# Which weight halves get their low part by accumulating DMA, by GpSimd or by VectorE, and when the conditioning loads are queued

## The chip, the cores and the metric

One core of one Trainium2 chip. The metric is the device time of one execution in microseconds. Three runs of the kernel before took 2086.33, 2087.24 and 2091.59 us (median 2087.24).

## The reference

Two decoder layers on a sequence of 256 tokens with model width 1024. Each layer has a conditioning part, a mixer and an expert part:

```python
mod = cond @ w_mod[l] + b_mod[l]                       # 6 x 1024 numbers from the conditioning vector
h = rms_norm(x, norm1_g[l]) * (1.0 + sc1) + sh1
x = x + g1 * hybrid_mixer(h, w_in[l], w_out[l], ...)   # attention, two convolutions, spatial gating
h = rms_norm(x, norm2_g[l]) * (1.0 + sc2) + sh2
x = x + g2 * peer_ffn(h, ...)                          # 8 heads, 16 of 128*128 one-neuron experts each
```

`peer_ffn` computes queries (`h @ wq`), scores them against 2 x 128 keys per head, takes the 16 best pairs per head and adds up `gate * gelu(h . u[e]) * v[e]` over the chosen experts e. All data are float32.

## The kernel before, in words

**Weights as a stream.** All weights of a layer are a list of tiles of 128 x 1024 float32 (512 KB): 20 of `win`, 8 of `wout`, 16 of `wq`, 128 of `u`, 128 of `v`. The kernel computes all 16384 experts densely: the "up" stage multiplies h with every `u` tile and takes gelu, gates (zero for experts not chosen) are multiplied in, and the "down" stage multiplies with every `v` tile.

**High and low parts.** TensorE multiplies in a shortened format (fp32r), so that each tile is cut into `hi` (the tile rounded) and `lo` (tile minus `hi`), and each product is three matmuls: hi*hi, hi*lo, lo*hi (`mm3`, L362 to L364 in the mixer, query and up stages; L928 in the down stage). The third one, L364, is the first to need `lo`.

**Class `Stream`** does this, by halves of 512 columns. `load` (L175) queues the 512 KB load of `raw` on SyncE; there are 4 `raw` buffers. `split_halves` (L179 to L210) makes `hi` and `lo` of one half; there are 6 buffers of each, three tiles' worth. It chooses one of three ways, per tile (both halves alike):

- "dve": ScalarE copies `raw` to `hi` (L200), VectorE subtracts (L202).
- "pool": ScalarE copies `raw` to `hi` (L200), GpSimd subtracts (L202 too).
- "dma": ScalarE writes `-raw`, rounded to fp32r, to `lo` (L196); a DMA that GpSimd issues adds `raw` to it (L197), which leaves the low part; ScalarE copies `raw` to `hi` (L198).

The share of tiles that goes each way is set stage by stage in `self.stream.share`: `MIXSHARE` in the mixer and query stages, `SHARE[0]` in the first half of up (64 tiles), `SHARE[1]` in the second half of up, `SHARE[2]` in the first half of down, `SHARE[3]` in the second half of down, and `{"dma": 1.0}` for the first two tiles of the program. What neither "dma" nor "pool" takes is VectorE's. The split runs 5 halves ahead of the multiplication (`AHEAD`).

**What runs beside the matmuls.** Class `Background` places slices of other work between the tiles: with each tile it advances its own clock by `STEP`, and a slice is emitted when VectorE's planned work is not more than `LEAD` ahead. A VectorE low part is charged with `LOCOST` = 0.6 us (`charge`). In the first half of up this other work is the choice of the experts (`topk`: MAX8, FIND_INDEX8, MATCH_REPLACE8 at L788 to L792, the 256 candidate sums per head at L799, one-hot products at L815 to L821), and in layer 0 also 16 conditioning chunks. In the second half of up and the first half of down it is the gates (`gates`: VectorE compares and products at L866 to L874, matmuls at L879, L887). In the second half of down of layer 0 it is 40 conditioning chunks of layer 1.

**Conditioning** (`mod_tiles`): a chunk is a load of 128 x 1025 float32 (L280, SyncE's queue, as the weights) and one VectorE SCALAR_TENSOR_TENSOR with a sum (L286). With n buffers, n-1 loads are queued first; after the instruction for chunk i the load of chunk i+n-1 follows, into the buffer of chunk i-1, and then the generator yields.

**Order.** Emission order is a priority. The framework's scheduler lets an instruction that it takes to be ready pass one that still waits; on each engine and queue the order that it fixed is then kept at run time, so that a waiting entry holds up what stands behind it, on SyncE's queue and on GpSimd's too.

At the start (`start`, L1021 on) GpSimd multiplies x by its norm (L1060, 8 instructions) and makes the low parts of h (L1073, 7 of 8); VectorE runs 16 conditioning chunks; the first two `win` tiles are split in between.

Of the kernel before, what the change touches and what calls it, by code (L numbers as in the profile page):

```python
# [15 lines left out]
ALU = mybir.AluOpType  # L16
# [21 lines left out]
MODCOST = 1.2  # L38
LOCOST = 0.6
HALF = D // 2  # L40
# [5 lines left out]
KTAKE = 3  # L46
CONVRANK = 2.5
PACE = (1.0, 2.6)
SHARE = ({"dma": 0.3, "pool": 0.7}, {"dma": 0.25}, {"dma": 0.2}, {"dma": 0.1})
NCOL = 94  # L50
NROW = 64 + 256 + 256 + 128
CH_SLICES = (4, 3, 0, 1, 7, 6, 5)
# [101 lines left out]
class Stream:  # L154
# [24 lines left out]
    def split_halves(self, upto):  # L179
        nc = self.nc  # L180
        while self.ns <= min(upto, 2 * len(self.aps) - 1):
            n, k = divmod(self.ns, 2)
            if k == 0:
                self.load(n)
                self.parts[n] = ([], [])
                self.by = "dve"
                for way in ("dma", "pool"):
                    self.acc[way] += self.share.get(way, 0.0)
                    if self.by == "dve" and self.acc[way] >= 1.0:
                        self.acc[way] -= 1.0  # L190
                        self.by = way
            raw = self.raw[n][:, HALF * k:HALF * k + HALF]
            hi = self.pool.tile([P, HALF], F32R, name="hi", tag="hi", bufs=6)
            lo = self.pool.tile([P, HALF], F32R, name="lo", tag="lo", bufs=6)
            if self.by == "dma":
                nc.scalar.activation(out=lo, in_=raw, func=AF.Copy, scale=-1.0)  # L196
                nc.gpsimd.dma_start(out=lo, in_=raw, accum_op=ALU.add)  # L197
                nc.scalar.activation(out=hi, in_=raw, func=AF.Copy)  # L198
            else:
                nc.scalar.activation(out=hi, in_=raw, func=AF.Copy)  # L200
                eng = nc.gpsimd if self.by == "pool" else nc.vector
                eng.tensor_tensor(out=lo, in0=raw, in1=hi.bitcast(F32), op=ALU.subtract)  # L202
                if self.by == "dve":
                    self.bg.charge(LOCOST)
            self.parts[n][0].append(hi)
            self.parts[n][1].append(lo)
            self.ns += 1
            if k:
                del self.raw[n]
                self.load(n + self.depth)  # L210
# [9 lines left out]
class Trunk:  # L220
# [52 lines left out]
    def mod_tiles(self, l, chunks, sc, bufs, tail=True, pace=0.0):  # L273

        nc = self.nc
        n = len(bufs)

        def load(i):
            if i < len(chunks):
                nc.sync.dma_start(out=bufs[i % n], in_=self.io["wmod"][l, chunks[i]])  # L280

        for i in range(n - 1):
            load(i)
        for i, j in enumerate(chunks):
            w = bufs[i % n]
            nc.vector.scalar_tensor_tensor(out=w, in0=w, scalar=1.0, in1=sc, op0=ALU.mult, op1=ALU.mult,  # L286
                                           accum_out=self.modT[:, l, j:j + 1])
            load(i + n - 1)
            yield MODCOST, pace
        for j0 in (8, 32):  # L290
            if tail and j0 in chunks:
                m = self.modT[:, l, j0:j0 + 8]
                g = self.col(l, 0 if j0 == 8 else 8, 8)
                nc.vector.scalar_tensor_tensor(out=m, in0=m, scalar=1.0, in1=g, op0=ALU.add, op1=ALU.mult)
                yield 0.2
# [64 lines left out]
    def mm3(self, out, whi, wlo, hhi, hlo, start, stop):  # L360
        mm = self.nc.tensor.matmul
        mm(out, whi, hhi, start=start, stop=False)  # L362
        mm(out, whi, hlo, start=False, stop=False)  # L363
        mm(out, wlo, hhi, start=False, stop=stop)  # L364
# [574 lines left out]
    def experts(self, l, area):  # L939
# [13 lines left out]
        acts = [self.big(32, T) for _ in range(2)]  # L953
        self.stream.share = SHARE[0]
        run = self.up(hb, acts)
        next(run)
        self.stream.share = SHARE[1]
        acts += [self.big(32, T) for _ in range(2)]
# [5 lines left out]
        for i in range(2):  # L964
            self.bg.add(self.gates(1, acts[2:4], i, kept))
        self.stream.share = SHARE[2]
        run = self.down(acts)
        next(run)
        self.stream.share = SHARE[3]
        self.m = Carve(self.big(), self.big())  # L970
# [50 lines left out]
    def start(self):  # L1021

        nc, io, one = self.nc, self.io, self.one
        self.cols = one.tile([P, L * NCOL + 8], F32, name="cols")
        self.ident = one.tile([P, P], F32, name="ident")
        self.xT = one.tile([P, NC, T], F32, name="xT")
        self.ones = one.tile([P, P], F32, name="ones")
        self.eps = one.tile([P, 1], F32, name="eps")
        self.iota = one.tile([P, P, 2], FP16, name="iota")
        self.modT = one.tile([P, L, 48], F32, name="modT")  # L1030
        self.idx = one.tile([P, 2, T], FP16, name="idx")
        self.gidx = one.tile([P, 2 * T], FP16, name="gidx")
        nc.vector.memset(self.ones, 1.0)
        nc.vector.memset(self.eps, EPS)
        self.neghalf = one.tile([P, 8], F32, name="neghalf")
        nc.vector.memset(self.neghalf, -0.5)
        self.m = m = Carve(self.big(), self.big())
        self.m2 = Carve(self.big())
        row = m.take(D)
        nc.sync.dma_start(out=row[0:1], in_=io["crow"])  # L1040
        nc.sync.dma_start(out=self.cols, in_=io["cols"])
        for i in range(2):
            nc.sync.dma_start(out=self.xT[:, 4 * i:4 * i + 4], in_=io["xT"][:, 4 * i:4 * i + 4])
        cr = self.m2.take(D + 1)
        for i in range(2):
            b = self.bank()
            nc.tensor.matmul(b, self.ones[0:1], row[0:1, 512 * i:512 * i + 512], start=True, stop=True)
            nc.scalar.activation(out=cr[:, 512 * i:512 * i + 512], in_=b, func=AF.Silu)
        nc.vector.memset(cr[:, D:D + 1], 1.0)
        bufs = [self.m2.take(D + 1) for _ in range(6)]  # L1050
        mods = self.mod_tiles(0, [j for c in range(NC) for j in (c, 8 + c)], cr, bufs, tail=False)
        next(mods)
        rs = self.rstd_d(m)
        self.stream.depth = 0
        self.stream.share = {"dma": 1.0}
        self.stream.split(1)
        r = self.bias_rows()
        xa, a = m.take(NC, T), m.take(2, T)
        for c in range(NC):
            nc.gpsimd.tensor_tensor(out=xa[:, c], in0=self.xT[:, c], in1=rs, op=ALU.mult)  # L1060
        hhi, hlo = hb = [self.mid(NC, T, dt=F32R) for _ in range(2)]
        for c in range(NC):
            for _ in range(2 if c else 1):
                next(mods)
            sh, sc = self.modT[:, 0, c:c + 1], self.modT[:, 0, 8 + c:9 + c]
            nc.vector.tensor_scalar(out=sc, in0=sc, scalar1=1.0, scalar2=self.col(0, c, 1), op0=ALU.add, op1=ALU.mult)
            nc.scalar.activation(out=hhi[:, c], in_=xa[:, c], func=AF.Identity, scale=sc, bias=sh)
            if c < NC - 1:
                nc.scalar.activation(out=a[:, c % 2], in_=xa[:, c], func=AF.Identity, scale=sc, bias=sh)
            else:  # L1070
                nc.vector.tensor_scalar(out=a[:, c % 2], in0=xa[:, c], scalar1=sc, scalar2=sh, op0=ALU.mult, op1=ALU.add)
            eng = nc.gpsimd if c < NC - 1 else nc.vector
            eng.tensor_tensor(out=hlo[:, c], in0=a[:, c % 2], in1=hhi[:, c].bitcast(F32), op=ALU.subtract)  # L1073
        for _ in mods:
            pass
        self.stream.load(3)
        self.stream.depth = self.stream.RAW
        nc.sync.dma_start(out=self.ident, in_=io["consts"][:, 0:P])
        m.reset()
        self.bias = m.take(4, 256)  # L1080
        self.table = self.bg.add(self.bias_table(r), rank=-1)
        self.bg.pump(0.1)
        self.mods = self.mod_tiles(0, list(range(16, 40)), cr, bufs[0:WBUFS])
        return hb
# [101 lines left out]
```

## Time and profile before

| what | value |
|---|---|
| median of three runs | 2087.24 us |
| the profiled execution's own time | 2079.62 us |
| its span | 2077.8 us |
| mean granted TensorE clock | 0.961 |
| PE busy | 1908.0 us, 92% |
| VectorE busy | 1432.6 us, 69% |
| ScalarE busy | 1155.0 us, 56% |
| GpSimd busy | 537.2 us, 26% |
| low parts by VectorE / GpSimd / DMA | 732 / 178 / 290 |

Busy time is time in which an engine had an instruction running. For the matmul engine, idle time in a stage, with what ended it, says what the stage waited for. A granted clock under 1.0 means that the matmuls themselves ran longer.

### The profile page before, as it was taken

Reading aid. Unit: us, or ns where it says so; the run is one execution under the profiler, and the core shown is the slowest. Engines: PE = TensorE matmul, PEld = TensorE weight load, DVE = VectorE, ACT = ScalarE, POOL = GpSimd, SP = SyncE. Lnnn points to the kernel's source line nnn. Section 1 sums busy time; section 2 is a strip of 40 time slices with the busy share of each in tenths; the row PEclk is TensorE's granted clock in tenths of the full one; section 3 lists DMA queues with packets and bytes.
Section 4 is the critical chain, followed back from the end, with each engine's and each line's share of the span. In section 5 each row is a group of like instructions: output and inputs, shape, how many; then the busy total and the mean of one; then the engine's idle time right before and its main releaser. Section 6 shows DMA issues by size and latency. Waiting matters only on the chain. (4 is left out here: it accounts for less than half of the span.)

```text
span 2077.8 us, 38198 instructions
## 1 busy us (share of the span) xinstructions
PE 1908.0 (92%) x13718; PEld 1720.2 (83%) x13718; DVE 1432.6 (69%) x3280; ACT 1155.0 (56%) x2329; POOL 537.2 (26%) x513
## 2 busy tenths in 40 slices
PE   4877987899999998889999989999999999999998
PEld 3777887889999886667787889999999988878886
DVE  6787799344666687666557877993477668855555
ACT  4565653465555554444557776666555555555554
POOL 4121265772111110000002223777411111110001
PEclk7988998899999999999999999999999999999999
DMA  8886877887888888898766767887888788877673
GB/s 289 256 254 204 223 198 223 260 229 218 249 244 255 255 256 287 279 295 284 225 211 168 206 167 204 238 219 219 234 262 243 245 255 271 261 207 220 210 212 113
DMA packets 164735, 485.59 MB, mean 234 GB/s; under 512 B 18588, under 2 KB 19905, under 8 KB 164290
## 3 DMA queue, kind: packets, MB, share of 16 engines
q1 hardware_dynamic: 122786, 407.13, 56.9%
q0 software_dynamic: 41760, 76.04, 20.9%
q8 instruction: 107, 1.75, 0.3%
q14 instruction: 82, 0.67, 0.1%
HBM read 388.72 MB, written 18.36 MB: 196 GB/s over the span
## 5 line engine op out<-in xcount | busy, mean ns | idle before, releaser
L364 PE MATMUL bank<-mid,lo 128*128 128x256 f32 x2432 | 702.3, 289 | 61.1 <-DMA lo<-raw 59.1
L200 ACT ACTIVATE hi<-raw 128x512 fp32r<-128x512 f32 x910 | 543.6, 624 | 323.4 <-PE bank L363 192.5
L362 PE MATMUL bank<-mid,hi 128*128 128x256 f32 x2432 | 704.5, 290 | 13.5 <-ACT hi L200 6.7
L363 PE MATMUL bank<-mid,hi 128*128 128x256 f32 x2432 | 695.5, 286 | 8.9 <-POOL mid L1073 8.9
L202 DVE TENSOR_TENSOR lo<-raw,hi 128x512 fp32r<-128x512 f32 x732 | 485.0, 688 | 204.5 <-ACT hi L200 200.1
L197 POOL DMA_DIRECT2D lo<-raw x290 | 253.2, 894 | 1390.6 <-PE acc L928 651.6
L928 PE MATMUL acc<-hi,mid 128*128 128x512 f32 x2048 | 570.0, 396 | 0.1
L364 PEld LDWEIGHTS bank<-mid,lo 128*128 128x128 f32 x2432 | 474.8, 195 | 72.0 <-DMA lo<-raw 69.2
L362 PEld LDWEIGHTS bank<-mid,hi 128*128 128x128 f32 x2432 | 475.1, 196 | 18.1 <-ACT hi L200 7.1
L363 PEld LDWEIGHTS bank<-mid,hi 128*128 128x128 f32 x2432 | 475.3, 196 | 9.5 <-POOL mid L1073 9.2
L928 PEld LDWEIGHTS acc<-hi,mid 128*128 128x128 f32 x2048 | 386.2, 191 | 78.4 <-ACT mid L913 0.4
L928 PE MATMUL acc<-lo,mid 128*128 128x512 f32 x1024 | 328.4, 398 | 31.5 <-DMA lo<-raw 31.2
L913 ACT ACTIVATE mid<-big 128x256 fp32r<-128x256 f32 x256 | 106.0, 415 | 307.8 <-PE acc L928 307.2
L928 PEld LDWEIGHTS acc<-lo,mid 128*128 128x128 f32 x1024 | 195.0, 190 | 84.5 <-DMA lo<-raw 44.2
L202 POOL TENSOR_TENSOR lo<-raw,hi 128x512 fp32r<-128x512 f32 x178 | 249.9, 1516 | 45.1 <-ACT hi L200 42.1
L198 ACT ACTIVATE hi<-raw 128x512 fp32r<-128x512 f32 x290 | 181.3, 625 | 134.7 <-PE bank L363 65.3
L914 DVE TENSOR_TENSOR mid<-big,mid 128x256 fp32r<-128x256 f32 x256 | 107.8, 423 | 199.0 <-PE acc L928 143.2
L196 ACT ACTIVATE lo<-raw 128x512 fp32r<-128x512 f32 x290 | 179.4, 621 | 57.8 <-PE acc L928 50.1
L286 DVE SCALAR_TENSOR_TENSOR big<-big 128x1025 f32<-128x1025 f32 x96 | 128.9, 1352 | 64.1 <-DMA big<-wmod 56.5
L874 DVE TENSOR_TENSOR og<-o,gidx 128x512 f16<-128x512 f16 x256 | 101.5, 436 | 0.2
L898 ACT ACTIVATE big<-bank 128x256 f32<-128x256 f32 x256 | 93.9, 367 | 0.0
L879 PEld LDWEIGHTS <-o 128*128 128x128 f16 x2048 | 67.4, 97 | 18.6 <-issue 12.3
(203 smaller groups left out, 1617.0 us busy)
## 6 DMA issues: line engine op xcount, KB each, us to landing
raw<-u SPq DMA_DIRECT2D x256, 512.0 KB, 4.6
raw<-v SPq DMA_DIRECT2D x256, 512.0 KB, 4.4
lo<-raw POOLq DMA_DIRECT2D x290, 256.0 KB, 5.0
big<-wmod SPq DMA_DIRECT2D x96, 512.5 KB, 6.5
raw<-win SPq DMA_DIRECT2D x40, 512.0 KB, 4.7
raw<-wq SPq DMA_DIRECT2D x32, 512.0 KB, 4.4
kept<-o SPq DMA_DIRECT2D x64, 256.0 KB, 5.2
o<-kept SPq DMA_DIRECT2D x64, 256.0 KB, 4.5
```

What stands on the lines that cost most here:

```text
L196: nc.scalar.activation(out=lo, in_=raw, func=AF.Copy, scale=-1.0)
L197: nc.gpsimd.dma_start(out=lo, in_=raw, accum_op=ALU.add)
L198: nc.scalar.activation(out=hi, in_=raw, func=AF.Copy)
L200: nc.scalar.activation(out=hi, in_=raw, func=AF.Copy)
L202: eng.tensor_tensor(out=lo, in0=raw, in1=hi.bitcast(F32), op=ALU.subtract)
L286: nc.vector.scalar_tensor_tensor(out=w, in0=w, scalar=1.0, in1=sc, op0=ALU.mult, op1=ALU.mult, accum_out=self.modT[:, l, j:j + 1])
L362: mm(out, whi, hhi, start=start, stop=False)
L363: mm(out, whi, hlo, start=False, stop=False)
L364: mm(out, wlo, hhi, start=False, stop=stop)
L913: nc.scalar.activation(out=a[:, 0], in_=src, func=AF.Copy)
L914: nc.vector.tensor_tensor(out=a[:, 1], in0=src, in1=a[:, 0].bitcast(F32), op=ALU.subtract)
L928: nc.tensor.matmul(self.acc[2 * tt + d], a[:, s, P * tt:P * tt + P], w[:, 512 * d:512 * d + 512], start=i == 0 and s == 0 and w is whi, st ...
```

## The change

Four edits. The accumulating DMA reads its half of the weight tile from DRAM, not from `raw` in SBUF. The shares change: the first half of up goes from 0.3 DMA and 0.7 GpSimd to 0.6 GpSimd and the rest VectorE, the first half of down from 0.2 to 0.15 DMA, the second half of down from 0.1 DMA to none, and the first two tiles of the program from DMA to VectorE; the mixer's share (0.4) and the second half of up (0.25) stay. In `mod_tiles` the yield stands before the next load, not behind it.

```diff
-SHARE = ({"dma": 0.3, "pool": 0.7}, {"dma": 0.25}, {"dma": 0.2}, {"dma": 0.1})
+SHARE = ({"pool": 0.6}, {"dma": 0.25}, {"dma": 0.15}, {})
@@ split_halves
             if self.by == "dma":
                 nc.scalar.activation(out=lo, in_=raw, func=AF.Copy, scale=-1.0)
-                nc.gpsimd.dma_start(out=lo, in_=raw, accum_op=ALU.add)
+                nc.gpsimd.dma_start(out=lo, in_=self.aps[n][:, HALF * k:HALF * k + HALF], accum_op=ALU.add)
                 nc.scalar.activation(out=hi, in_=raw, func=AF.Copy)
@@ mod_tiles
             nc.vector.scalar_tensor_tensor(out=w, in0=w, scalar=1.0, in1=sc, op0=ALU.mult, op1=ALU.mult,
                                            accum_out=self.modT[:, l, j:j + 1])
+            yield MODCOST, pace
             load(i + n - 1)
-            yield MODCOST, pace
@@ start
-        self.stream.share = {"dma": 1.0}
+        self.stream.share = {}
         self.stream.split(1)
```

## Rows read from the trace of the kernel before

**Rows 1.** The page, part 1: busy us, share of the span, instructions.
```profile
PE 1908.0 (92%) x13718; PEld 1720.2 (83%) x13718; DVE 1432.6 (69%) x3280; ACT 1155.0 (56%) x2329; POOL 537.2 (26%) x513
```

**Rows 2.** Waits (us in total, times, longest), and those of line 364 alone.
```profile
PE bank L364 <- DMA lo<-raw: 59.1, 36, 5.9
...
PE acc L928 <- DMA lo<-raw: 31.2, 23, 3.6
...
  POOL lo L202: 2.8, 4
  DVE lo L202: 0.9, 3
```

**Rows 3.** Windows by stage: us; PE, PEld, DVE, ACT, POOL busy; clock; DMA share; GB/s.
```profile
252.20:485.70 233.50, 199.99 (x1531) 196.02 (x1530) 152.21 (x374) 119.11 (x234) 152.39 (x127) 0.93 0.78 228
...
691.40:916.70 225.30, 204.20 (x1270) 161.75 (x1271) 170.89 (x375) 109.50 (x222) 21.95 (x26) 0.96 0.86 274
916.70:1107.40 190.70, 180.58 (x770) 146.71 (x768) 117.36 (x217) 102.36 (x209) 12.05 (x14) 0.97 0.77 241
...
1290.30:1485.50 195.20, 187.31 (x1531) 185.38 (x1530) 138.76 (x342) 121.25 (x233) 150.68 (x126) 0.99 0.81 222
...
1689.80:1885.00 195.20, 193.74 (x1271) 156.87 (x1272) 144.15 (x322) 107.04 (x220) 22.19 (x26) 1.00 0.82 245
1885.00:2062.00 177.00, 175.94 (x771) 143.79 (x770) 99.03 (x174) 98.39 (x200) 10.46 (x12) 1.00 0.65 195
```

**Rows 4.** Groups of PE: up 252:486 and 1290:1486, then down 691:917 and 917:1107.
```profile
L364 PE MATMUL bank<-mid,lo 128*128 128x256 f32 x509 | 151.3, 297 | 26.5 <-DMA lo<-raw 25.4 <-POOL lo L202 1.1
...
L364 PE MATMUL bank<-mid,lo 128*128 128x256 f32 x509 | 145.8, 287 | 7.9 <-DMA lo<-raw 7.7
...
L928 PE MATMUL acc<-lo,mid 128*128 128x512 f32 x256 | 85.0, 409 | 19.6 <-DMA lo<-raw 19.6
...
L928 PE MATMUL acc<-lo,mid 128*128 128x512 f32 x256 | 82.6, 400 | 10.1 <-DMA lo<-raw 10.1
```

**Rows 5.** Tile lo: low parts of each way, duration ns min/median/max, and landing of the DMAs.
```profile
L202 DVE TENSOR_TENSOR lo<-raw,hi x732: 627/687/1229, 42.1 to 2054.9; 128x512 fp32r<-128x512 f32 x183
...
L197 POOL DMA_DIRECT2D lo<-raw x290: 851/869/1879, 33.5 to 2033.2; - x145
L202 POOL TENSOR_TENSOR lo<-raw,hi x178: 1262/1448/3345, 256.7 to 1484.6; 128x512 fp32r<-128x512 f32 x178
...
DMA to landing us min/median/max: 3.3/5.0/10.5
```

**Rows 6.** Timeline of one wait in the up stage of layer 0 (start us, us).
```profile
370.15 0.62 ACT L196 ACTIVATE lo<-raw 128x512 fp32r<-128x512 f32 x1
...
371.33 1.76 POOL L197 DMA_DIRECT2D lo<-raw  x2
...
379.91 0.58 PE L364 MATMUL bank<-mid,lo 128*128 128x256 f32 x1 [5.75 <-DMA lo<-raw]
```

**Rows 7.** Line 799: durations over the span, its group in 1290:1486, one instance beside GpSimd.
```profile
L799 DVE TENSOR_TENSOR big<-big x32: 394/768/5639, 254.1 to 1378.6; 128x256 f32<-128x256 f32 x32
...
L799 DVE TENSOR_TENSOR big<-big 128x256 f32<-128x256 f32 x16 | 34.2, 2139 | 0.0
...
1325.20 5.36 POOL L202 TENSOR_TENSOR lo<-raw,hi 128x512 fp32r<-128x512 f32 x4
...
1325.46 5.39 DVE L799 TENSOR_TENSOR big<-big 128x256 f32<-128x256 f32 x1
```

**Rows 8.** Waits of SyncE's queue (us in total, times, longest).
```profile
SPq L175 <- DMA lo<-raw: 693.4, 132, 13.4
...
SPq L280 <- DVE big L286: 35.0, 16, 8.1
```

**Rows 9.** Timelines of GpSimd and of PE at the start, 30 to 40 us.
```profile
33.45 3.68 POOL L197 DMA_DIRECT2D lo<-raw  x4
...
38.19 0.58 PE L364 MATMUL bank<-mid,lo 128*128 128x256 f32 x1 [5.71 <-DMA lo<-raw]
```

## The prediction

> **What bounds the kernel now.** First the page: TensorE is busy for 1908 of 2077.8 us, VectorE for 1433 [rows 1]. TensorE is the bound, and what can be won is its idle time and the time that its matmuls lose at a low clock. Second the waits: PE waited 59.1 us at L364 and 31.2 us at L928 for accumulating DMAs, 90.3 us together; at L364 only 2.8 us went to low parts of GpSimd and 0.9 us to those of VectorE [rows 2]. VectorE makes 732 low parts, GpSimd 178, the DMAs 290 [rows 5]: not even a quarter of the low parts cause nearly all the waiting.
>
> Third, where. The windows stand in pairs: first half of up, first and second half of down, in layer 0 and then layer 1 [rows 3]. The same tiles take 233.5 and 195.2 us in up, 225.3 and 195.2, 190.7 and 177.0 us in down: layer 0 loses 82 us against layer 1. It is the layer in which conditioning chunks are loaded in these stages. Idle time of PE is 33.5 against 7.9 us in up (span less busy), 21.1 against 1.5 and 10.1 against 1.1 us in down [rows 3]. Of these, 25.4, 7.7, 19.6 and 10.1 us (the last two in layer 0) were ended by an accumulating DMA [rows 4]. The rest of layer 0's loss is longer matmuls: PE is busy for 200.0 against 187.3 us in up at clocks of 0.93 and 0.99, for 204.2 against 193.7 at 0.96 and 1.00, for 180.6 against 175.9 at 0.97 and 1.00 [rows 3].
>
> Last, why the DMA is late. In the timeline, ScalarE has the negated half at 370.77, GpSimd issues two DMAs from 371.33, and PE goes on at 379.91 after 5.75 us of idleness [rows 6]. The raw data had been there before 370.15, so it is the second transfer that is late: 8.6 us behind the issue, where the median landing is 5.0 and the longest 10.5 us [rows 5]. With `hi` first and a subtraction of 0.69 us behind it [rows 5], this half would have been ready near 371.5, before PE's wait began at 374.16.
>
> **The change part by part.**
>
> *Counts.* First half of up: 2 layers x 64 tiles x 2 halves = 256 halves; 0.3 of them are 76 accumulating DMAs, which all go; GpSimd's go from 178 to 0.6 x 256, 152 after rounding, so VectorE gets some 104, 52 a layer. First half of down: 256 x 0.05, 12 DMAs go. Second half: 256 x 0.1, 26 go. Start: 4 go. So 118 of 290 go, 172 stay, and VectorE has 144 more.
>
> *Up, layer 0.* The 25.4 us of idleness goes, and of the 12.7 us of longer matmuls (200.0 less 187.3) a share of 25.4/33.5, 9.6 us: -35. Some of it comes back where `raw` itself is late behind conditioning loads: +3, bounds 0 and 8 (the idle time of this stage that no accumulating DMA ends, 33.5 less 25.4).
>
> *Up, layer 1.* -7.7, and about 1 of clock: -9.
>
> *What VectorE then costs in up.* It is busy for 152.2 and 138.8 us there [rows 3] and gets 52 x 0.69 = 36 more: 188 of about 205, 175 of 195. That is nearly full, and it is in order: a low part stands behind `topk`. This kernel shows a further price. L799 takes 0.39 us at its shortest, but 2.14 on average in this stage; one instance lasts 5.39 us, from 1325.46 to 1330.85, beside four GpSimd subtractions from 1325.20 to 1330.56 [rows 7]. So a VectorE instruction with two SBUF inputs is held while GpSimd subtracts. The new low parts are such instructions. Sixteen L799 cost 16 x 1.75 = 28 us a layer now. GpSimd's own load falls: 38 DMA issues of 0.87 us and 13 subtractions of 1.45 us a layer go [rows 5], 52 us of its 151, so I scale the 28 to about 19. For 26 new pairs of halves the bounds are 0 (VectorE comes in a pause of GpSimd's) and 26 x 1.75 = 45 us; I take 15, a third, because GpSimd stops by itself when the six buffers are full, and about half of it while `topk` runs. Late are then 19 + 8 = 27 us; buffers of three tiles give two tiles of 2.9 us, 6 us, of slack, and the planner makes room by its 0.6 us a half. So 0 to 21 us of PE idleness a layer; I take 12, twice: +24.
>
> The Trainium skill ("SBUF — State Buffer", section "Who interferes with whom") says that a VectorE instruction with two SBUF inputs and a GpSimd instruction that reads SBUF exclude each other, the second one blocking until the first has ended. The rows of L799 agree. Taken strictly, that rule speaks against this part of the change.
>
> *First half of down.* In layer 0 a quarter of the accumulating DMAs goes: 19.6 x 0.25 = 5 us, and a quarter of 10.5 us of clock, 2: -7. Layer 1: 0. VectorE gets 6 halves a layer, 4 us, in stages where it is idle for 51 us and more [rows 3].
>
> *Second half of down.* Layer 0: -10.1 and the 4.7 us of clock: -14. Layer 1: -1. VectorE, busy for 117.4 of 190.7 us, gets 13 x 0.69 = 9 us a layer; GpSimd has no subtraction there that could hold it.
>
> *Start.* GpSimd issues the four DMAs for 3.68 us from 33.45, between low parts of h, and PE waits 5.71 us for the first [rows 9]. VectorE's four subtractions, 2.8 us, lie between conditioning chunks. PE then follows GpSimd's low parts of h, so I take -4, bounds 0 and -7.
>
> *DRAM source, 172 DMAs.* `raw` comes free when ScalarE has read it, and the queue of loads no longer waits for these DMAs (693.4 us of its waits now [rows 8]); this shows in PE's time only where `raw` is late. Against it, 172 x 0.26 MB more is read from DRAM. No row has an accumulating DMA from DRAM. What stays exposed is 90.3 - 25.4 - 7.7 - 19.6 x 0.25 - 10.1 - 5.7, about 36 us; a landing longer or shorter by a third bounds it at 12 us either way. I take 0: it moves the same bytes into the same buffer.
>
> *Loads a slice later.* SyncE's queue waits 35.0 us for L286 now [rows 8], with weight loads behind it. In a run of chunks the order stays (load, next chunk), elsewhere other work comes between. Bounds: -10, and +10 if the last eight chunks of the mixer of layer 0 each come a planned slice of 1.2 us later. I take 0.
>
> *Sum.* -35 + 3 - 9 + 24 - 7 - 14 - 1 - 4 = -43 us. The profiled execution took 2079.6 us (span 2077.8) and gives 2037; the median, 2087.24, lies 7.6 higher and gives 2044. I write 2043.
>
> **The rivals.**
>
> *VectorE becomes the bound of up (slower).* Place: L202 on VectorE in the first half of up. Price: if each of the 52 halves is held for 1.75 us as L799 is, VectorE needs 138.8 + 36 + 91 = 266 us in layer 1 for a stage of 195, and 152.2 + 36 + 91 = 279 in layer 0 for one of 233.5: +71 and +46, less the 26 us won elsewhere: 2178. It decides from a hold of about 0.9 us a half, where both stages together lose the 26 us. For it: rows 7, and 175 of 195 us filled without any hold. Against it: GpSimd loses a third of its work, and PE has hardly ever waited for VectorE's low parts. Chance 0.14.
>
> *Pairs held (no change).* Held once per pair, 45 us: VectorE needs 220 and 233 us, layer 1 loses 25, layer 0 wins nothing, and the rest is won: about 2087. Chance 0.08.
>
> *The data are late anyway (small gain).* If, in layer 0, DRAM traffic is what delays, `hi` becomes the wait where the DMA was, and only a quarter of the idleness goes: about 2073. Rows 6 speak against it: the data were there. Chance 0.08.
>
> **How the numbers follow.** The forecast, a gain of 25 to 75 us, has 0.70. A measurement of this kernel can tell 0.3%, 6 us, from no change. Faster: 0.70 + 0.08 = 0.78. Same: 0.08. Slower: 0.14. The range: its low end is the sum without VectorE's 24 us and with 10 from the unknown terms, 2010; the high end takes in the small gain and the case of no change, 2093. It leaves out the slower case and a still larger gain, 0.2 together.
>
> **What would show it.** Right: PE's waits for `lo<-raw` DMAs at L364 and L928 fall from 90 to about 35 us and are gone from the first half of up; layer 0's first half of up takes near 210 us and its second half of down near 177; the clock there returns to 0.97 or more. Wrong: PE waits for VectorE's L202 in up, with L202's longest durations at several us and VectorE's busy share near full; or `hi` waits for `raw` in layer 0 where the DMA was awaited; or the mixer's remaining accumulating DMAs land later than 5.0 us.

## The result: 1.4% slower

| kernel | median, us | runs | ratio to before, 95% interval |
|---|---|---|---|
| before | 2087.14 | 4 | 1 |
| after | 2117.96 (2110.05 to 2121.20) | 4 | 1.0138 (1.0106 to 1.0169) |

The forecast was 2043, a gain; the kernel lost 31 us. The profiled execution of after took 2118.32 us (span 2116.6), 38.7 more than that of before. First the page, part 1 (busy us, share of the span, instructions), which answers to [rows 1]:

```profile
PE 1920.2 (91%) x13718; PEld 1728.6 (82%) x13718; DVE 1511.3 (71%) x3424; ACT 1106.2 (52%) x2215; POOL 442.3 (21%) x369
```

TensorE still is the bound and does the same work in 12 us more of busy time; the rest of the loss is idle time. VectorE has the 144 further low parts (x3424 against x3280), GpSimd 144 instructions fewer.

**Where the time went.** The stages from the same matmul to the same matmul in every trace; a column is one profiled execution (us; the tail of some 16 us is left out). The experiments' columns are used further below.

| stage | before | after | e2 | e4 | e13 | e12 |
|---|---|---|---|---|---|---|
| start and mixer, layer 0 | 126.2 | 121.9 | 118.9 | 128.3 | 119.8 | 117.3 |
| output and queries, layer 0 | 126.1 | 122.7 | 119.5 | 131.1 | 122.9 | 119.9 |
| up, first half, layer 0 | 233.5 | 207.5 | 206.8 | 209.1 | 208.6 | 191.2 |
| up, second half, layer 0 | 205.7 | 217.4 | 205.7 | 203.4 | 205.6 | 206.0 |
| down, first half, layer 0 | 225.3 | 232.5 | 220.1 | 224.8 | 220.8 | 192.3 |
| down, second half, layer 0 | 190.7 | 181.6 | 179.9 | 179.9 | 181.9 | 179.6 |
| mixer, layer 1 | 80.0 | 93.7 | 87.3 | 92.0 | 88.2 | 83.8 |
| output and queries, layer 1 | 102.8 | 111.7 | 105.0 | 119.4 | 106.2 | 108.7 |
| up, first half, layer 1 | 195.2 | 202.6 | 204.9 | 203.8 | 205.3 | 189.2 |
| up, second half, layer 1 | 204.3 | 215.7 | 205.1 | 203.8 | 202.7 | 204.7 |
| down, first half, layer 1 | 195.2 | 219.4 | 196.8 | 201.4 | 197.8 | 192.2 |
| down, second half, layer 1 | 177.0 | 174.3 | 174.2 | 174.3 | 174.3 | 174.2 |

A stage differs by some us between single traces even where no edit touches it: the first half of up of layer 1 takes 195.2 us here and 200.3 in the trace of e3 below.

The stages from which the accumulating DMAs were taken moved about as forecast: -26 and +7 in the first half of up, -9 and -3 in the second half of down, -4 at the start. From the second half of up of layer 0 on, the stages that kept some lost: +12 and +11 in the second half of up, +7 and +24 in the first half of down, +14 and +9 in the mixer and queries of layer 1. Windows of before, second half of up of layer 0 and mixer of layer 1, which the prediction did not look at (columns as in [rows 3]):

```profile
485.70:691.40 205.70, 203.37 (x2055) 200.82 (x2053) 135.90 (x286) 113.26 (x226) 27.49 (x33) 1.00 0.81 247
1107.40:1187.50 80.10, 71.46 (x498) 64.36 (x497) 71.97 (x174) 59.69 (x128) 18.80 (x21) 0.98 0.70 182
```

And of after: first half of up, second half of up, first half of down of layer 0; mixer and first half of down of layer 1.

```profile
244.50:452.00 207.50, 191.56 (x1533) 188.43 (x1532) 185.63 (x425) 100.54 (x194) 130.88 (x76) 0.98 0.59 205
452.00:669.40 217.40, 205.53 (x2052) 201.00 (x2050) 136.39 (x285) 114.84 (x226) 27.68 (x32) 1.00 0.81 234
669.40:901.90 232.50, 205.61 (x1270) 163.47 (x1271) 172.65 (x378) 107.18 (x217) 17.26 (x20) 0.95 0.79 254
...
1083.60:1177.30 93.70, 77.65 (x496) 68.96 (x496) 73.76 (x175) 62.95 (x130) 19.03 (x21) 0.89 0.60 153
...
1707.30:1926.70 219.40, 200.95 (x1270) 160.18 (x1271) 147.26 (x327) 104.75 (x215) 17.49 (x20) 0.98 0.71 214
```

The second half of up issues as many accumulating DMAs as before, and VectorE and ScalarE do the same work there, yet PE idles for 11.9 us where it idled for 2.3. In the first half of down of layer 1 its idle time goes from 1.5 us [rows 3] to 18.5, and in the mixer the clock goes from 0.98 to 0.89 on top.

PE's waits in after (us in total, times, longest), which answer to [rows 2]:

```profile
PE acc L928 <- DMA lo<-v: 42.0, 23, 4.0
...
PE bank L364 <- DVE lo L202: 28.9, 26, 3.5
...
PE bank L364 <- DMA lo<-u: 20.5, 23, 2.0
...
PE bank L364 <- DMA lo<-win: 13.3, 6, 5.6
...
PE bank L364 <- DMA lo<-wq: 11.5, 7, 4.4
```

The transfers now carry the name of the weight that they read. At these two lines PE waited 87.3 us for 172 accumulating DMAs, and had waited 90.3 for 290. The landing of those DMAs, in the view of tile `lo`, answers to [rows 5]:

```profile
DMA to landing us min/median/max: 3.7/6.8/11.1
```

The median went from 5.0 to 6.8 us. SyncE's queue, which answers to [rows 8]:

```profile
SPq L175 <- DVE lo L202: 997.7, 361, 12.0
...
SPq L175 <- ACT lo L196: 86.8, 45, 4.6
```

The 693.4 us for which weight loads had waited for an accumulating DMA are gone; instead a load follows the last instruction that reads `raw`, in a "dma" tile ScalarE's. One such tile in the second half of up of layer 0 (timeline: start us, us):

```profile
550.02 0.86 POOL L197 DMA_DIRECT2D lo<-u  x1 [11.42 <-DVE og L874]
...
551.46 3.14 SPq L175 DMA_DIRECT2D raw<-u  x2
551.73 0.86 POOL L197 DMA_DIRECT2D lo<-u  x1 [0.84 <-PE bank L364]
...
558.75 0.39 PE L364 MATMUL bank<-mid,lo 128*128 128x256 f32 x1 [0.66 <-DMA lo<-u]
```

ScalarE read the second half of this tile last. A 512 KB load goes out at 551.46, between the two accumulating DMAs, and PE goes on 7.0 us after the second one was issued.

### The profile page after: what moved, and what is told of

It reads as the page before. It is cut to its first block, busy times and chain, and to the rows that moved or that the text cites. A ratio compares the mean times of both kernels' runs of the same rounds, so it can differ in the third digit from the quotient of the medians.

```text
span 2116.6 us, 37772 instructions
## 1 busy us (share of the span) xinstructions
PE 1920.2 (91%) x13718; PEld 1728.6 (82%) x13718; DVE 1511.3 (71%) x3424; ACT 1106.2 (52%) x2215; POOL 442.3 (21%) x369
## 3 DMA queue, kind: packets, MB, share of 16 engines
q8 instruction: 107, 1.75, 0.3%
## 4 chain that ended last, share of the span: by engine, by line
PE 41%; issue 25%; DMA 16%; DVE 13%; ACT 2%; POOL 2%; POOLq 0%; SPq 0%; DVEq 0%; ACTq 0%
PE acc L928 17%; PE bank L364 7%; DMA lo<-u 7%; PE bank L362 7%; PE bank L363 7%; DVE lo L202 3%; DMA lo<-v 2%; DMA lo<-win 2%; DMA lo<-wq 2%; DMA big<-wmod 2%; POOL lo L197 1%; PE acc L879 1%; DVE big L789 1%; DVE big L790 1%; DVE big L792 1%
## 5 line engine op out<-in xcount | busy, mean ns | idle before, releaser
L202 DVE TENSOR_TENSOR lo<-raw,hi 128x512 fp32r<-128x512 f32 x876 | 614.6, 726 | 290.0 <-ACT hi L200 285.1
L364 PE MATMUL bank<-mid,lo 128*128 128x256 f32 x2432 | 705.1, 290 | 74.1 <-DVE lo L202 28.9
L928 PE MATMUL acc<-hi,mid 128*128 128x512 f32 x2048 | 572.6, 398 | 0.1
L364 PEld LDWEIGHTS bank<-mid,lo 128*128 128x128 f32 x2432 | 474.4, 195 | 89.4 <-DVE lo L202 35.0
L928 PEld LDWEIGHTS acc<-hi,mid 128*128 128x128 f32 x2048 | 388.3, 192 | 79.5 <-ACT mid L913 0.4
L928 PE MATMUL acc<-lo,mid 128*128 128x512 f32 x1024 | 328.5, 399 | 42.1 <-DMA lo<-v 42.0
L202 POOL TENSOR_TENSOR lo<-raw,hi 128x512 fp32r<-128x512 f32 x152 | 245.4, 1628 | 176.7 <-ACT hi L200 163.8
L928 PEld LDWEIGHTS acc<-lo,mid 128*128 128x128 f32 x1024 | 196.0, 191 | 93.0 <-DMA lo<-v 52.2
L197 POOL DMA_DIRECT2D lo<-u x66 | 57.4, 870 | 378.0 <-ACT lo L196 152.9
L197 POOL DMA_DIRECT2D lo<-v x40 | 34.8, 875 | 420.9 <-PE acc L928 345.5
L196 ACT ACTIVATE lo<-raw 128x512 fp32r<-128x512 f32 x172 | 105.6, 621 | 29.2 <-PE acc L928 25.0
L874 DVE TENSOR_TENSOR og<-o,gidx 128x512 f16<-128x512 f16 x256 | 96.4, 417 | 0.2
```

Of the source, the lines that this page charges most:

```text
L197: nc.gpsimd.dma_start(out=lo, in_=self.aps[n][:, HALF * k:HALF * k + HALF], accum_op=ALU.add)
L928: nc.tensor.matmul(self.acc[2 * tt + d], a[:, s, P * tt:P * tt + P], w[:, 512 * d:512 * d + 512], start=i == 0 and s == 0 and w is whi, st ...
```

## The experiments

Two theories of the loss, called A1 and A2 here and in the expectations. **A1, order:** with the source in SBUF, `raw` stayed taken until the DMA had read it, and that kept the next load out of the DMA's way; with the source in DRAM the load is queued first. **A2, DRAM:** an accumulating DMA that reads DRAM takes longer by itself. In the expectations of e1 to e3, "Theory A" means either of the two; their rivals B and C are the new shares and the later conditioning loads. Beside them stands a question of [rows 7]: whether VectorE in the first half of up is slowed by its own load or by GpSimd's subtractions.

**e1_dram_only.** The kernel before with the DRAM source alone.

```diff
-                nc.gpsimd.dma_start(out=lo, in_=raw, accum_op=ALU.add)
+                nc.gpsimd.dma_start(out=lo, in_=self.aps[n][:, HALF * k:HALF * k + HALF], accum_op=ALU.add)
```

> The kernel before with one edit: its 290 accumulating DMAs read DRAM instead of raw. Theory A (the DRAM source is what cost the time, by whatever way): the stages that kept their DMAs lost some 64 us with 172 of them, so with 290 it is slower than before by 60 to 110 us, 2150 to 2200, and the median landing rises from 5.0 to over 6 us. Rival B (the shares did it: VectorE and GpSimd hold each other in the first half of up): no change, 2081 to 2093, landing near 5.

2224.68 us, 1.0649 (1.0608 to 1.0690): the edit costs 138 us with 290 DMAs, more than was expected. The median landing is 6.5 us, and PE's waits for `lo<-v` at L928 alone are 78.9 us.

**e2_sbuf_back.** The kernel after with the SBUF source (that line the other way round).

> The changed kernel with the accumulating DMAs reading raw in SBUF again. Theory A: the 64 us come back, 2040 to 2065, faster than the kernel before by 20 to 45 us; landing near 5 us; second half of up near 205 us in both layers. Rival B: still slower than before, 2105 to 2120.

2041.54 us, 0.9781 (0.9747 to 0.9815): all the rest of the change together is worth -45 us, and the source costs 76. The stages that kept accumulating DMAs come back to before's times within some 2 us or better, but for the mixer of layer 1 (87.3 against 80.0). SyncE's queue in e2:

```profile
SPq L175 <- DVE lo L202: 657.3, 292, 12.0
SPq L175 <- DMA lo<-raw: 539.8, 85, 14.1
```

The loads wait for the DMAs again, and PE waits less for them: 20.6 us at L364 and 20.2 at L928, in place of 45.3 and 42.0. Idle time in this queue was no loss.

**e3_loads_only.** The kernel before with the later conditioning loads alone.

```diff
-            load(i + n - 1)
             yield MODCOST, pace
+            load(i + n - 1)
```

> The kernel before with one edit: the conditioning loads are queued a slice later. Theory A and rival B: no change, 2081 to 2093. Rival C (the later loads cost time in layer 0): slower by 10 us or more.

2082.00 us, 0.9963 (0.9933 to 0.9993): about 5 us won, hardly more than noise. In the profiled execution, which took 2087.10 us as a whole, the output and query stage of layer 0 has 122.0 us in place of 126.1.

**e4_dram_held.** After, with a reason for `raw` to stay taken: GpSimd reads one column of `raw` and of the finished low part of each half, so that the buffer comes free only when the DMA has landed.

```diff
+                if self.by == "dma":
+                    j = self.pool.tile([P, 2], F32, name="junk", tag="junk", bufs=2)
+                    for q in range(2):
+                        nc.gpsimd.tensor_tensor(out=j[:, q:q + 1], in0=self.raw[n][:, HALF * q:HALF * q + 1],
+                                                in1=self.parts[n][1][q][:, 0:1].bitcast(F32), op=ALU.add)
                 del self.raw[n]
```

> The changed kernel, DRAM source kept, but raw is held until both accumulating DMAs of its tile have landed: two additions of one column on GpSimd read raw and lo into a scratch tile that nothing uses. Theory A1 (raw free early: the next 512 KB load is queued ahead of the accumulating DMA and its packets go first): weight loads within 2 us of an accumulating DMA fall from 2.5 to 3 back to about 0.5, landing to 4.5 to 5.5 us, the time to 2045 to 2070. Theory A2 (reading the source in DRAM itself is late): landing stays at 6 to 8 us and the time at 2105 to 2130.

2089.56 us, 1.0016 (0.9996 to 1.0035): 28 us better than after, less than was expected, and the median landing of 6.0 us did not come back to 5.5. Second half of up and first half of down, layer 0 and then layer 1:

```profile
468.50:671.80 203.30, 202.43 (x2054) 200.63 (x2052) 136.08 (x286) 114.58 (x226) 38.96 (x64) 1.00 0.86 247
671.80:896.60 224.80, 206.75 (x1270) 163.65 (x1271) 171.91 (x378) 107.15 (x217) 25.72 (x38) 0.95 0.83 266
1491.70:1695.50 203.80, 202.93 (x2054) 200.76 (x2053) 137.19 (x286) 114.10 (x225) 37.57 (x64) 1.00 0.85 249
1695.50:1897.00 201.50, 195.07 (x1271) 156.78 (x1272) 147.06 (x327) 104.69 (x215) 26.42 (x40) 1.00 0.75 226
```

Still read from DRAM, these four stages take 833 us; they took 885 in after and take 828 in e2. Of 57 us lost there 52 come back by the hold alone. A timeline of the second half of up shows the order that it restores (L212 are the additions that hold the buffer):

```profile
561.20 0.88 POOL L197 DMA_DIRECT2D lo<-u  x1 [4.62 <-PE bank L368]
...
562.90 0.86 POOL L197 DMA_DIRECT2D lo<-u  x1 [0.83 <-ACT lo L196]
...
565.44 3.25 SPq L175 DMA_DIRECT2D raw<-u  x2
...
566.36 0.44 POOL L212 TENSOR_TENSOR junk<-raw,lo 128x1 f32<-128x1 f32 x1 [2.59 <-issue]
568.14 0.19 POOL L212 TENSOR_TENSOR junk<-raw,lo 128x1 f32<-128x1 f32 x1 [1.35 <-DMA lo<-u]
```

The next load leaves 2.5 us behind the issue of the second DMA, not between the two, and the one into this tile's own buffer, the second of that row, behind the last addition. In the mixer and query stages e4 is 40 us slower than e2 (sum of four rows of the table), and in sum slower than after too: there GpSimd, which has norms and low parts of h to do, now waits 173 us in order for landings. What DRAM itself costs in those stages can't be read from e4.

**e6_tiny_hold.** The hold by a third GpSimd DMA of two columns of `raw`, queued behind the two.

```diff
+                if k:
+                    j = self.pool.tile([P, 2], F32, name="junk", tag="junk", bufs=2)
+                    nc.gpsimd.dma_start(out=j, in_=self.raw[n][:, 0:2])
```

> The changed kernel, DRAM source kept, raw held in another way: behind the two accumulating DMAs of a tile GpSimd issues a third, of two columns, that reads raw into a scratch tile that nothing uses, so that raw comes free about when they have landed and no engine waits. It tells whether the mixer and query stages, where the hold by additions on GpSimd won nothing, lost to that hold's own waiting. Theory A1 alone (early loads collide): every stage comes back, 2040 to 2070, mixer and query stages of layer 1 within 5 us of those with the SBUF source (87 and 105 us). Theory A1 in the up and down stages and A2 (DRAM reads land later) in the mixer: 2070 to 2095, those two stages stay 8 us or more longer.

2123.45 us, 1.0174 (1.0135 to 1.0213): as after, outside both expectations. The small DMA landed 3.6 us after its issue (median), the accumulating ones 6.9: it read `raw` long before they were done and held nothing back. The run tells only that a DMA behind others on this queue is no fence.

**e10_queue_hold.** The hold on SyncE's queue: two DMAs of two columns from the finished low parts back into `raw`.

```diff
+                if self.by == "dma":
+                    for q in range(2):
+                        nc.sync.dma_start(out=self.raw[n][:, HALF * q:HALF * q + 2],
+                                          in_=self.parts[n][1][q][:, 0:2].bitcast(F32))
                 del self.raw[n]
```

> The changed kernel, DRAM source kept, raw held by SyncE's own queue: behind the accumulating DMAs of a tile two DMAs of two columns copy from lo back into raw, so that the next load into this buffer waits for the landing, as it did before the change, and GpSimd waits for nothing. Theory A1 alone: landing falls to about 5 us in all stages, second half of up to 205, and the mixer and query stages of layer 1 (93.7 and 111.7 us in the changed kernel) to within 5 us of 87 and 105: 2040 to 2065. Theory A1 in up and down and A2 (DRAM reads land later) in mixer and queries: those two stages stay 6 us or more longer, 2070 to 2095.

2130.56 us, 1.0204 (1.0166 to 1.0241), slower than after: a miss. The whole queue stands behind these entries:

```profile
SPq L211 <- DMA lo<-u: 261.0, 60, 9.5
```

so that the loads come in bursts of three or four ahead of the next accumulating DMA, and the second half of up takes 226.8 us. This hold has a price of its own and decides nothing between A1 and A2.

**e13_first_half_dram.** After, with the first half of each tile read from DRAM and the second from `raw`: 86 DMAs still read DRAM, but the buffer stays taken until the second has read it.

```diff
+                nc.gpsimd.dma_start(out=lo, in_=raw if k else self.aps[n][:, 0:HALF], accum_op=ALU.add)
```

> The changed kernel, but only the first half of a tile is added from DRAM, the second half from raw, so that raw is held as it was before the change without any extra instruction. Theory A1 (it is the next weight load, let in between the two accumulating DMAs, that makes the second one late): the second half lands near 5.9 us on average again (7.7 in the changed kernel, 5.9 with the SBUF source), the first near 5.5 although it reads DRAM, second half of up near 205 us, mixer and query stages of layer 1 near 87 and 105, the time 2036 to 2055. Theory A2 (DRAM reads land later, above all in the mixer): first halves land 1 us or more later than with the SBUF source (over 6.5), 2060 to 2085.

2054.88 us, 0.9851 (0.9785 to 0.9917), just inside the range of A1. By A2 half of the 76 us should have stayed; against e2 13 did. In the table the four stages of the second half of up and the first half of down take 827 us, as in e2: there half of the DRAM reads cost nothing that shows. Counted from the traces: the mean landing of first and of second halves (us); then how many second halves had a load, weight or conditioning, issued from 1.5 us ahead of them to 0.5 us behind, and the mean landing of these and of the others.

| kernel | first | second | second halves with a load near | their landing | the others' |
|---|---|---|---|---|---|
| before | 5.34 | 5.60 | 25 of 145 | 7.6 | 5.2 |
| e2, SBUF | 5.53 | 5.91 | 13 of 86 | 8.1 | 5.5 |
| e13, first from DRAM | 5.85 | 6.27 | 17 of 86 | 8.0 | 5.9 |
| e4, DRAM and hold | 6.03 | 6.56 | 22 of 86 | 8.4 | 5.9 |
| after, DRAM | 5.98 | 7.66 | 82 of 86 | 7.6 | 8.3 (four of them) |

What after does to the second half, the one behind which the buffer is freed early, is 1.75 us over e2, and only 0.45 to the first. The counts say why: with a load near, a second half lands after 7.6 to 8.4 us whichever source it reads; in after nearly all have one, with the SBUF source or a hold a quarter at most. Of all 290 DMAs of before, the 226 with at most one load issued from 3 us ahead of them to 1 us behind land after 5.0 us on average, and those with two, three, and four or five after 6.4, 7.4 and 8.9. That coarser count alone doesn't explain after: at the same number of loads its DMAs land some 0.9 us later than those of e2. It is the load just ahead of the second half that came in.

The counts also show why e4 won nothing in the mixer and query stages: 16 of its 22 second halves with a load near lie there, of 33.

**The first half of up: load or hold?** Four kernels with other shares.

```diff
-SHARE = ({"dma": 0.3, "pool": 0.7}, {"dma": 0.25}, {"dma": 0.2}, {"dma": 0.1})
+SHARE = ({"pool": 0.6}, {"dma": 0.25}, {"dma": 0.2}, {"dma": 0.1})
```

is **e8_up_share_only** (otherwise the kernel before).

> The kernel before with one edit: the first half of up takes 0.6 GpSimd and the rest VectorE. From the stages of the changed kernel: layer 0 wins some 26 us, layer 1 loses 7 to 10, so 2087 less 17: 2062 to 2078. Rival B (VectorE and GpSimd hold each other, a loss on balance): 2095 or more.

2072.53 us, 0.9926 (0.9903 to 0.9948): the stage takes 211.8 and 205.2 us in the two layers. Layer 0 wins 22; layer 1 loses 10 against the trace of before, 5 against that of e3.

```diff
-        self.stream.share = SHARE[0]
+        self.stream.share = SHARE[0] if l == 0 else {"dma": 0.3, "pool": 0.7}
```

is **e7_layer1_old_share** (otherwise e2).

> The changed kernel with the SBUF source, and in layer 1's first half of up the old share (0.3 DMA, 0.7 GpSimd). The new share cost that stage 7 to 10 us (195.2 to 202.6 and 204.9) where no conditioning load disturbs it, so I expect 2041 less 8 to 10: 2028 to 2037. If the price of the new share is made good elsewhere: 2038 to 2045.

2033.04 us, 0.9737 (0.9702 to 0.9773): 8 us better than e2, but the stage itself went only from 204.9 to 202.8 us, the rest from stages that the edit doesn't touch. The total was as expected, the place was not: with the shares of before, the stage doesn't come back to 195.2 us.

**e9_up_no_pool** is e2 with no GpSimd low parts in that stage, so that VectorE makes all 128 of a layer:

```diff
-SHARE = ({"pool": 0.6}, {"dma": 0.25}, {"dma": 0.15}, {})
+SHARE = ({}, {"dma": 0.25}, {"dma": 0.15}, {})
```

> The changed kernel with the SBUF source and no subtraction on GpSimd: VectorE makes all low parts of the first half of up (128 halves, 88 us a layer). If it is the hold by GpSimd that makes PE wait for VectorE there (29 us now): L799 falls to 0.40 us and L202 to 0.69, PE's wait falls under 15 us, the time to 2025 to 2045. If it is VectorE's load: PE's wait grows to over 40 us and layer 1's stage to over 210 us, the time to over 2055.

2016.94 us, 0.9661 (0.9620 to 0.9702), 25 us better than e2 and faster than expected. The stage takes 189.5 and 189.1 us, 17 and 16 less than in e2, although VectorE makes 2.5 times as many low parts in it. (Of these 33 us, 11 come back in the second half of up, which takes 212.1 and 209.2 us; 5 of the 11 are idle time of PE, the rest busy time.) PE's waits in the stage in layer 0, first in e2, then, two lines, in e9 (L830 is PE's own part of the expert choice):

```profile
L364 PE MATMUL bank<-mid,lo 128*128 128x256 f32 x509 | 147.6, 290 | 15.6 <-DVE lo L202 15.6
...
L364 PE MATMUL bank<-mid,lo 128*128 128x256 f32 x509 | 145.2, 285 | 1.4 <-DVE lo L202 1.4
...
L830 PE MATMUL bank<-ident,big 128*128 128x128 f32 x4 | 1.0, 293 | 2.3 <-DVE big L821 1.8 <-DVE big L826 0.5
```

L799 of e9 over the whole span (duration in ns: min, median, max):

```profile
L799 DVE TENSOR_TENSOR big<-big x32: 394/408/421, 239.8 to 1321.5; 128x256 f32<-128x256 f32 x32
```

and, in the view of tile `lo`, VectorE's low parts:

```profile
L202 DVE TENSOR_TENSOR lo<-raw,hi x1028: 627/685/1227, 18.8 to 1993.9; 128x512 fp32r<-128x512 f32 x172
```

L799 had gone up to 5.64 us in before [rows 7] and to 1.51 in e2; with no GpSimd subtraction in the stage its longest is 0.42, and no low part of VectorE takes over 1.23 (1.79 in after). In layer 0 VectorE is busy for 324 us in both halves of up, in e2 for 322, with 76 more low parts of 0.69 us, 52 us: about 50 us of being held are gone. So the hold was the price, not VectorE's load. What the load costs is the 2.3 us a layer that PE now waits for the end of the expert choice (L821, L826). The Trainium skill ("SBUF — State Buffer", section "Who interferes with whom") says that of a VectorE instruction with two SBUF inputs and a GpSimd instruction that reads SBUF the later one waits for the other's end. That there is a hold agrees; its length doesn't: the L799 of 5.39 us in [rows 7] lasted through four subtractions, of which no single one in before takes over 3.35 us.

**e11_gates_one and e12_mixer_only** go on from e9 and drop the accumulating DMAs of the first half of down too, and e12 those of the second half of up:

```diff
-SHARE = ({}, {"dma": 0.25}, {"dma": 0.15}, {})
+SHARE = ({}, {"dma": 0.25}, {}, {})
...
+SHARE = ({}, {}, {}, {})
```

> SBUF source, no GpSimd subtraction, and no accumulating DMA in the first half of down either (VectorE makes 20 halves a layer more, 14 us, in stages of 220 and 197 us where it was busy for about 175 and 147). If what is left of DMA waits in layer 0 (16.7 us and its clock) goes: 2016 less 15 to 25, 1992 to 2003. If raw is late there or VectorE fills up: 2008 to 2025.

> As the run with one gate stage, and no accumulating DMA in the second half of up: only the mixer and query stages keep them. VectorE gets 32 halves a layer more there, 22 us, in stages of 205 to 214 us where it was busy for about 137. DMA waits of 4.6 and 2.4 us go: 3 to 8 us faster than the run with one gate stage, 1988 to 1998. If the leftover of the expert choice and the gates fill VectorE: slower than that run by 3 us or more.

1984.96 us, 0.9526 (0.9478 to 0.9573), and 1976.34 us, 0.9471 (0.9438 to 0.9505), the best kernel here; both are faster than expected. e12, both halves of up and of down of layer 0:

```profile
237.10:428.30 191.20, 186.48 (x1530) 184.52 (x1529) 176.36 (x480) 100.48 (x196) 0.00 (x0) 1.00 0.68 225
428.30:634.30 206.00, 203.95 (x2063) 202.07 (x2061) 165.88 (x338) 98.74 (x194) 0.00 (x0) 0.99 0.65 208
634.30:826.50 192.20, 192.20 (x1264) 157.10 (x1265) 177.35 (x393) 95.38 (x195) 0.00 (x0) 1.00 0.81 278
826.50:1006.10 179.60, 176.94 (x769) 143.63 (x768) 128.83 (x239) 95.52 (x195) 0.00 (x0) 1.00 0.74 245
```

In the first half of down PE has no idle time left and a full clock: 20 accumulating DMAs cost e2 28 us there (220.1 against 192.3), and the same between e9 and e11, which differ by this edit alone (220.9 against 192.4). VectorE, which makes every low part, is busy for 177 of the 192 us. The second half of up takes as long as in e2.

## Why the prediction was wrong, point by point

**The step that failed** is the term "DRAM source, 172 DMAs": "I take 0: it moves the same bytes into the same buffer", with bounds of 12 us either way. It measured +76 (after against e2), six times its bound; in the traces it is 77, of which 57 lie in the second half of up and the first half of down and 19 in the mixer and query stages. Two things failed in it. First the cause: the prediction had read [rows 8] and had said that `raw` would come free earlier and that the queue would no longer wait for these DMAs, but took this as a possible gain only. That wait of 693.4 us was what kept a load out of the accumulating DMA's way. For the 57 us this is shown by e4 and e13: with the hold back, 52 of them come back while all DMAs still read DRAM, and all of them while half do. The trace of before had it, and in the very wait that the prediction read in [rows 6]: beside the two accumulating DMAs issued from 371.33 us SyncE's queue issued a weight load and three conditioning loads.

```profile
371.42 0.33 SPq L175 DMA_DIRECT2D raw<-u  x1
371.80 2.02 SPq L280 DMA_DIRECT2D big<-wmod  x3
```

Second the bound: "a landing longer or shorter by a third" was about what came (a median of 5.6 us in e2, 6.8 in after, a fifth more), but the prediction let the exposed 36 us grow in the same proportion. What is exposed is only what of a landing sticks out over the slack of the buffers, and that more than doubled: PE's waits at L364 and L928 went from 40.8 to 87.3 us. Of the rest of the 77 us, 23 are longer matmuls (PE is busy for 1920.2 us, in e2 for 1897.2) and some 7 other idle time.

**What DRAM itself costs** is smaller: 0.3 to 0.4 us a landing and 13 us in all by e13, where half of the DMAs read it, and 0.5 to 0.65 us a landing by e4, whose hold has a price of its own. No run gives the total for all 172. In the mixer and query stages the two theories were not separated: of the 19 us lost there e13 wins back 13, and 29 of 33 second halves have a load near in after, 7 in e2 and 11 in e13, which speaks for the order; but 6 us stay.

**The rest of the sum held in total, in part by luck.** That term was taken as 0, so 2043 was also the forecast without it, and e2 took 2041.54. But against the trace of before, start, mixer and queries of layer 0 won 14 us in e2 where 4 were forecast, and in layer 1 the mixer and the first half of up lost 7 and 10 where 0 and 3 were. The parts, in after:

- *Counts:* 876, 152 and 172, as worked out.
- *Up, layer 0:* forecast -35 + 3 + 12 = -20, measured -26. The clock went to 0.98 ("0.97 or more"), the stage to 207.5 us ("near 210").
- *Up, layer 1:* forecast -9 + 12 = +3, measured +7.4.
- *VectorE in up:* 12 us of PE idleness a layer were forecast; the groups of L364 in the two layers show 15.9 and 13.0:

```profile
L364 PE MATMUL bank<-mid,lo 128*128 128x256 f32 x509 | 147.6, 290 | 15.9 <-DVE lo L202 15.9
...
L364 PE MATMUL bank<-mid,lo 128*128 128x256 f32 x509 | 146.9, 289 | 13.0 <-DVE lo L202 13.0
```

- The hold moved the way that was argued from [rows 7], with other sizes: in layer 1, L799 fell from 2.14 us to 0.73, and the new low parts took 0.91 on average where one alone takes 0.69. That is some 5 us of hold at L799 and 11 at the low parts, where the sum had 19 and 15; that the 12 us of idleness came out near is luck in part:

```profile
L202 DVE TENSOR_TENSOR lo<-raw,hi 128x512 fp32r<-128x512 f32 x50 | 45.1, 908 | 43.9 <-ACT hi L200 43.8
...
L799 DVE TENSOR_TENSOR big<-big 128x256 f32<-128x256 f32 x16 | 11.6, 728 | 0.0
```

- *Second half of down:* forecast -15, measured -9.1 and -2.7. *Start:* -4 and -4.3. *Loads later:* 0 within 10, e3 shows -5.
- *First half of down:* forecast -7; e2, which has this edit without the DRAM source, shows -5.2 and +1.6.

**The rivals.** The one that ended slower named VectorE in up, and its loss of 71 and 46 us did not come; the loss had another place and another cause. "Pairs held" had 45 us of hold a layer at the new low parts; 11 came. "The data are late anyway" fell: PE's wait in up went from the DMA to VectorE, not to `raw`. Of the signs listed as wrong, the mixer's DMAs landing later than 5.0 us came true (a median of 7.9 us for `lo<-win`), and everywhere else they did too; it was listed without a price. PE's wait for L202 in up came half: 28.9 us, near the 24 of the sum, with no L202 over 1.79 us. The sign listed as right, 90 us of waits falling to about 35, failed in after (87.3) and came in e2 (40.8).

**Open.** The mixer of layer 1 takes 87.3 us in e2 and 80.0 before; e8, which lacks the DRAM source and the later loads, has 84.8. No run explains these 5 to 7 us.

## What to carry to other kernels

A buffer that is held for long also paces what refills it. Before an edit frees a buffer earlier, ask which load starts earlier by it, and whose transfer on the critical path that load then runs beside. A low part by VectorE, 0.69 us in the median, beat here both a 256 KB transfer of 5 to 9 us and a GpSimd subtraction that holds VectorE, as long as VectorE had room.

## What the runs showed of the hardware

- An accumulating DMA's landing depended on the loads around it more than on its source: second halves with a load issued just ahead landed after 7.6 to 8.4 us, others, but for four, after 5.2 to 5.9. The Trainium skill ("DMA: Bandwidth & Descriptors", section "Queues, rings and completion order") says that each DMA engine takes turns between the queues that have work for it; these landings fit that, but no run here tests it.
- A two-column DMA behind two accumulating ones on GpSimd's queue landed in 3.6 us, ahead of theirs at 6.9.
- Beside GpSimd's subtractions one VectorE operation lasted up to 5.64 us in place of 0.40. With them gone, VectorE made all the stage's low parts and it became 16 to 17 us shorter.
